# A second matmul operand that holds norm and shift in the second block of a two-block transformer, on one core

## The chip, the cores and the metric

The kernel runs on one core of a Trainium2 chip. The metric is the device time of one execution in microseconds (us), the median of several runs. TensorE (PE in the rows) multiplies, VectorE (DVE), ScalarE (ACT) and GpSimd (POOL) work on vectors, and SyncE (SP) issues most DMA transfers.

## What is computed

Two transformer blocks run one after the other on 256 tokens of width 1024, with all numbers in float32. The change touches the second block alone. Cut to what matters, that block is:

```python
def rms_norm(x, w):
    y = xf * lax.rsqrt(jnp.mean(xf * xf, axis=-1, keepdims=True) + EPS)
    return y * w
def modulate(h, shift, scale):
    return h * (1.0 + scale[:, None, :]) + shift[:, None, :]

for layer in range(2):
    mod = silu_c @ ada_w[layer] + ada_b[layer]
    shift_m, scale_m, gate_m, shift_f, scale_f, gate_f = jnp.split(mod, 6, axis=-1)
    h = modulate(rms_norm(x, norm_mix_w[layer]), shift_m, scale_m)
    # layer 0: neighbourhood attention and a gated recurrence (HGRN2) of h @ ev_w_in
    # layer 1: (gate_b * dwconv3(gate_c * u)) of h @ od_w_in
    y = even_mixer(h, ...) if layer == 0 else short_conv_mixer(h, ...)
    x = x + gate_m[:, None, :] * y
    h = modulate(rms_norm(x, norm_ffn_w[layer]), shift_f, scale_f)
    a, val = jnp.split(h @ ffn_w_up[layer], 2, axis=-1)      # 2 x 2816 columns
    x = x + gate_f[:, None, :] * ((gelu(dwconv3(a)) * val) @ ffn_w_down[layer])
```

So four stages begin with a normed, scaled and shifted activation h that is multiplied by a wide weight matrix.

## The kernel before

Activations lie with the model width on the partitions: x is eight blocks (kt) of 128 rows by 256 tokens. A float32 product is made of three fast ones: both operands are split into a high half and a low remainder, and `mm3` (L117) multiplies high by high (L122), high by low (L123) and low by high (L124). `proj_fm` (L135) makes one output tile of 128 features: 8 kt by 3 are 24 matmuls into one PSUM bank. `load_w` (L105) brings the tile's weights, 128 x 1024, by a DMA of SP into one of four buffers; ACT casts the high half (L114) and DVE subtracts for the low half (L115), into one of three buffers named w.

The operand of the tiles (x2, from `hl_tiles`, two buffers) is not h. It holds x times the gain, without the norm, so that PE can start while the sum of squares is still under way; two further columns, 256 and 257, hold the shift and half of it (`put_shift`). A tile therefore has 258 columns. The norm comes behind the product: DVE multiplies the 258 columns by rstd (1 / root mean square, the same in all 128 rows; 1 in the last two columns), and a later instruction adds column 256 as a bias. rstd is copied from PSUM by ACT (L233).

The four stages and their tiles in program order are: mix2 (32 tiles; the first eight are the forget gates of four heads and two directions, L928 and L979, whose logarithms, scans and exponentials, L476, L1018 to L1058, are made together after the last of them), ffn2(0) (22 steps ft of two tiles, the gate g and the up-product u, L378 to L401), mix3 (8 steps of three tiles, L1270 to L1291) and ffn2(1) (as ffn2(0)). ada vectors (`ada_after`; 96 rows of w_ada, one DVE instruction each, L450) are made in between at a written pace. A scheduler with a timing model of its own sets each engine's order of instructions ahead of the run; each engine then works its row off in order. The PSUM banks that serve the tiles (three named acc, two named sc) and the three buffers of w decide how far tiles run ahead.

Of the kernel before, what the change touches and what calls it, by code (L numbers as in the profile page):

```python
# [16 lines left out]
P = 128  # L17
# [8 lines left out]
DOWN = ((0, 8), (8, 8), (16, 6))  # L26

# [23 lines left out]
def network(ctx: ExitStack, tc: tile.TileContext, a):  # L51
# [107 lines left out]
    def hl_tiles():  # L159
        return HL.of(hpool.tile([P, 2, KT, S + 2], F32R, tag="x2", name="x2"))  # L160
# [208 lines left out]
    def ffn(pool, w_up, w_dn, x2, rstd, conv, mod, down_evac, rates):  # L369


        n = S + 2 if mod else S
        a2 = HL.of(pool.tile([P, 2, FT, S], F32R, name="a2"))
        for ft in range(FT):
            pg = proj_fm(w_up[ft, 0], x2, n)
            pu = proj_fm(w_up[ft, 1], x2, n)
            g = pool.tile([P, S + 2], F32, tag="g", bufs=2, name="g")
            nc.vector.tensor_tensor(out=g[:, :n], in0=pg[:, :n], in1=rstd[:, :n], op=ALU.mult)  # L378
            cv = pool.tile([P, S], F32, tag="cv", bufs=2, name="cv")
            if mod:  # L380
# [22 lines left out]
            if rates[0] and ft % rates[0] == rates[0] - 1:  # L403
# [514 lines left out]
    for kt in range(KT):  # L918
        nc.vector.scalar_tensor_tensor(out=x[:, kt], in0=x[:, kt], scalar=col("final_g", kt),
                                       in1=rx[:, :S], op0=ALU.mult, op1=ALU.mult)  # L920

    NM = S + 2
    with tc.tile_pool(name="mix2", bufs=1, reuse_waits="tile") as pool:
# [24 lines left out]
        y2 = hl_tiles()  # L948
# [22 lines left out]
        class Head:  # L971
# [16 lines left out]
            def project(self):  # L988
# [4 lines left out]
                gated(raw(12 + h), self.hq)  # L993
                t = raw(24 + h)
                plus_shift(t, t[:, :S])
                to_tokens(t[:, :S], self.v)
                gated(raw(28 + h), self.gg)
# [212 lines left out]
    def ffn2(l, gain, rates):  # L1210
        nxt = hl_tiles() if gain is not None else None
        sq = SumSq()

# [26 lines left out]
        def down_evac(nt, ps):  # L1240
            if not nxt:
                return final_evac(nt, ps)
            if nt == 0:
                gain_of(col("norm_mix_w_2", 8, 8), m(1, 1), gain)
                put_shift(nxt, m(1, 0))
# [4 lines left out]
            split(nxt, nt, x[:, nt], gain[:, nt : nt + 1])  # L1250
# [13 lines left out]
    with tc.tile_pool(name="mix3", bufs=1, reuse_waits="tile") as pool:  # L1264
# [7 lines left out]

        for ft in range(KT):
            tc_ = raw3(8 + ft)
            tu = raw3(16 + ft)
            nc.scalar.activation(tu[:, :S], tu[:, :S], AF.Identity, bias=tu[:, S : S + 1])
            cu = pool.tile([P, S], F32, tag="cu", bufs=2, name="cu")
            nc.vector.scalar_tensor_tensor(out=cu, in0=tc_[:, :S], scalar=tc_[:, S : S + 1],
                                           in1=tu[:, :S], op0=ALU.add, op1=ALU.mult)
# [3 lines left out]
            for i, so, si in ((0, slice(1, S), slice(0, S - 1)), (2, slice(0, S - 1), slice(1, S))):  # L1283
# [118 lines left out]
```

## Time and profile before

| | |
|---|---|
| time, median of 3 runs (lowest, highest) | 1372.6 us (1370.77, 1374.56) |
| the profiled execution: own time, span | 1373.04 us, 1371.3 us |
| PE, DVE, ACT, POOL busy | 98%, 82%, 61%, 4% |
| chain that ended last | PE 93% |
| mean granted clock of TensorE | 0.997 |

The span is what the trace covers of the execution; the rest of its own time lies around it. A busy share is the time in which an instruction of the engine runs over the span. The chain is followed back from the last instruction to whatever released it. Start times in rows are microseconds from the span's start.

### The profile page before, as it was taken

The page shows a single profiled execution, that of the slowest core. Times are in us where ns is not written, and L with a number is a line of the kernel's source. Part 1 is how long each engine was busy: PE and PEld are TensorE (multiplying, and loading weights), DVE is VectorE, ACT ScalarE, POOL GpSimd, SP SyncE. Part 2 cuts the span into 40 slices and gives each one's busy share as a digit, 9 for nine tenths or more (in the row PEclk, how much of TensorE's full clock was granted, in tenths as well). Part 3 has the DMA queues.
Part 4 walks back from the last instruction along what each step waited for, and adds up shares of the span by engine and source line. Part 5 has one row for each costly group of instructions (what it writes and reads, how often), then busy time and mean ns, then how long its engine had stood idle before and what let it go on. Part 6 is the DMA issues. An engine that isn't in the chain of part 4 may idle for free.

```text
span 1371.3 us, 26850 instructions
## 1 busy us (share of the span) xinstructions
PE 1342.9 (98%) x10482; PEld 1283.1 (94%) x10482; DVE 1119.4 (82%) x2125; ACT 829.9 (61%) x1444; POOL 51.0 (4%) x72
## 2 busy tenths in 40 slices
PE   8999999999999999999998999999999999999997
PEld 7998999999999999999898987899998999999986
DVE  7887799997775968999888976789989898888854
ACT  7756665555566765555557766666654455666653
POOL 1000000000101000000030110000000000000000
PEclk9999999999999999999999999999999999999999
DMA  7753667766655557888875453367779875656563
GB/s 261 249 176 109 221 224 223 228 208 195 207 161 156 197 186 250 279 271 275 269 232 179 148 166 122 125 216 231 227 221 324 288 248 187 195 184 185 177 185 100
DMA packets 79696, 284.19 MB, mean 207 GB/s; under 512 B 8912, under 2 KB 9040, under 8 KB 79440
## 3 DMA queue, kind: packets, MB, share of 16 engines
q1 hardware_dynamic: 78480, 278.67, 62.8%
q0 software_dynamic: 800, 3.15, 0.7%
q8 instruction: 82, 1.34, 0.4%
q10 hardware_dynamic: 288, 0.66, 0.1%
q14 instruction: 46, 0.38, 0.1%
HBM read 281.39 MB, written 1.05 MB: 206 GB/s over the span
## 4 chain that ended last, share of the span: by engine, by line
PE 93%; DVE 2%; ACT 2%; DMA 1%; issue 1%; SPq 0%; POOLq 0%; POOL 0%; DVEq 0%; ACTq 0%
PE ps_acc L124 15%; PE ps_acc L122 15%; PE ps_acc L123 14%; PE ps_sc L124 7%; PE ps_sc L122 7%; PE ps_sc L123 7%; PE ps_acc L129 6%; PE ps_sc L129 4%; PE ps_acc L130 3%; PE ps_sc L130 2%; PE ps_sc L304 2%; PE ps_acc L156 1%; PE ps_acc L154 1%; PE ps_acc L155 1%; PE ps_att L343 1%
## 5 line engine op out<-in xcount | busy, mean ns | idle before, releaser
L114 ACT CAST w<-wraw 128x1024 fp32r<-128x1024 f32 (+2 forms) x438 | 445.7, 1023 | 400.1 <-PE ps_acc L124 152.9
L115 DVE TENSOR_TENSOR w<-wraw,w 128x1024 fp32r<-128x1024 f32 (+2 forms) x438 | 522.8, 1198 | 123.1 <-ACT w L114 119.1
L124 PE MATMUL ps_acc<-x,w 128*128 128x256 f32 (+1 forms) x1560 | 441.6, 284 | 3.2 <-DVE w L115 3.2
L122 PE MATMUL ps_acc<-x,w 128*128 128x256 f32 (+1 forms) x1560 | 442.1, 285 | 2.5 <-ACT w L114 1.7
L123 PE MATMUL ps_acc<-x,w 128*128 128x256 f32 (+1 forms) x1560 | 441.6, 283 | 0.0
L122 PEld LDWEIGHTS ps_acc<-x,w 128*128 128x128 f32 x1560 | 294.2, 189 | 6.8 <-ACT w L114 3.6
L124 PEld LDWEIGHTS ps_acc<-x,w 128*128 128x128 f32 x1560 | 294.3, 189 | 6.3 <-DVE w L115 4.2
L123 PEld LDWEIGHTS ps_acc<-x,w 128*128 128x128 f32 x1560 | 295.3, 189 | 2.3 <-issue 2.0
L122 PE MATMUL ps_sc<-x,w 128*128 128x256 f32 (+1 forms) x840 | 240.0, 286 | 8.9 <-ACT w L114 6.7
L124 PE MATMUL ps_sc<-x,w 128*128 128x256 f32 (+1 forms) x840 | 239.5, 285 | 0.0
L123 PE MATMUL ps_sc<-x,w 128*128 128x256 f32 (+1 forms) x840 | 239.0, 285 | 0.2 <-DVE x L170 0.2
L122 PEld LDWEIGHTS ps_sc<-x,w 128*128 128x128 f32 x840 | 160.3, 191 | 10.8 <-ACT w L114 7.3
L123 PEld LDWEIGHTS ps_sc<-x,w 128*128 128x128 f32 x840 | 160.7, 191 | 0.8 <-DVE x L166 0.4
L124 PEld LDWEIGHTS ps_sc<-x,w 128*128 128x128 f32 x840 | 160.3, 191 | 0.3 <-DVE w L115 0.2
L129 PE MATMUL ps_acc<-a,w 128*128 128x512 f32 x374 | 130.8, 390 | 0.0
L450 DVE CUSTOM_DVE_ANT_0 ada<-ada,cvec,vec 128x1024 f32<-128x1024 f32 x96 | 121.8, 1277 | 2.4 <-DMA ada<-w_ada 2.3
L130 PE MATMUL ps_acc<-a,w 128*128 128x256 f32 x374 | 105.7, 283 | 1.3 <-DVE w L115 1.3
L129 PE MATMUL ps_sc<-a,w 128*128 128x512 f32 x242 | 84.9, 390 | 0.0
L129 PEld LDWEIGHTS ps_acc<-a,w 128*128 128x128 f32 x374 | 70.2, 188 | 14.4
L389 DVE SCALAR_TENSOR_TENSOR cv<-g,vec,cv 128x255 f32<-128x255 f32 (+1 forms) x176 | 83.0, 476 | 0.4 <-ACT cv L387 0.3
L130 PEld LDWEIGHTS ps_acc<-a,w 128*128 128x128 f32 x374 | 70.6, 189 | 2.4 <-DVE w L115 2.0
L130 PE MATMUL ps_sc<-a,w 128*128 128x256 f32 x242 | 68.2, 282 | 0.0
(377 smaller groups left out, 1893.4 us busy)
## 6 DMA issues: line engine op xcount, KB each, us to landing
wraw<-w_up SPq DMA_DIRECT2D x176, 512.0 KB, 4.3
ada<-w_ada SPq DMA_DIRECT2D x96, 512.0 KB, 4.8
wraw<-w_dn SPq DMA_DIRECT2D x64, 512.0 KB, 4.2
wraw<-w_ev SPq DMA_DIRECT2D x44, 512.0 KB, 3.8
wraw<-w_dn SPq DMA_DIRECT2D x32, 384.0 KB, 4.1
wraw<-w_od SPq DMA_DIRECT2D x24, 512.0 KB, 4.4
wraw<-w_qk SPq DMA_DIRECT2D x12, 512.0 KB, 4.8
wraw<-w_aout SPq DMA_DIRECT2D x8, 512.0 KB, 3.6
```

The lines of the kernel that those rows point to most:

```text
L114: nc.scalar.copy(hi[:, c], raw[:, c])
L115: nc.vector.tensor_tensor(out=lo[:, c], in0=raw[:, c], in1=hi.bitcast(F32)[:, c], op=ALU.subtract)
L122: nc.tensor.matmul(ps, w.h[:, c], x.h[:, kt, :n], start=first, stop=False)
L123: nc.tensor.matmul(ps, w.h[:, c], x.l[:, kt, :n], start=False, stop=False)
L124: nc.tensor.matmul(ps, w.l[:, c], x.h[:, kt, :n], start=False, stop=last)
L129: nc.tensor.matmul(ps, w.h[:, c], x.both[:, :, kt, :n], start=first, stop=False)
L130: nc.tensor.matmul(ps[:, 0], w.l[:, c], x.h[:, kt, :n], start=False, stop=last)
L154: nc.tensor.matmul(ps, x.l[:, kt, t], v.h[:, c], start=kt == 0, stop=False)
L155: nc.tensor.matmul(ps, x.h[:, kt, t], v.h[:, c], start=False, stop=False)
L304: nc.tensor.matmul(sps[j][:, o : o + n], self.q[r, qt * P : (qt + 1) * P], kap[r], start=True, stop=True)
L389: nc.vector.scalar_tensor_tensor(out=cv[:, so], in0=g[:, si], scalar=conv(i, ft), in1=cv[:, so], op0=ALU.mult, op1=ALU.add)
L450: nc.vector.tensor_tensor_reduce(out=out, in0=wt, in1=cvec[j], scale=1.0, scalar=col("ada_b", 48 * l + n), op0=ALU.mult, op1=ALU.add, accu ...
```

## The change

Four stages get a second operand, xn, that holds norm, gain and shift already. `normed` makes it, one block kt per step: POOL multiplies x by rstd into a buffer nt (two of them), ACT applies gain and shift in place, ACT casts the high half and DVE subtracts for the low half. The first tiles of a stage still read x2 with 258 columns and are normed behind the product: eight in mix2, six in each of the others (RAW = 3). All later tiles read xn with 256 columns and are evacuated straight from PSUM: no multiplication by rstd, no bias. The steps of `normed` are written behind the first tiles: two after each head's forget gates, three after each of the first three ft, four after each of the first two steps of mix3. Operand rows stand 260 apart. In mix2 the eight instructions that turn x into x times final_g times its own norm move behind the steps of `normed`, since these read the x from before. In the up-projection of ffn2(0) one ada vector less is made.

The diff, cut to its core (line numbers of the kernel after are larger; L126 to L128 are the three matmuls, L118 and L119 cast and subtraction of the weights, L191, L192, L169 and L170 the four instructions of `normed`):

```diff
@@ -24,6 +24,10 @@
+
+SX = 260
+
+RAW = 3
...
@@ -157,7 +161,7 @@
     def hl_tiles():
-        return HL.of(hpool.tile([P, 2, KT, S + 2], F32R, tag="x2", name="x2"))
+        return HL.of(hpool.tile([P, 2, KT, SX], F32R, tag="x2", name="x2"))
...
@@ -179,6 +183,17 @@
+    def normed(x2, src, gain, shift, rstd):
+
+        def step(kt):
+            t = npool.tile([P, S], F32, tag="sst", name="nt")
+            nc.gpsimd.tensor_tensor(out=t, in0=src[:, kt], in1=rstd[:, :S], op=ALU.mult)
+            nc.scalar.activation(t, t, AF.Identity, scale=gain[:, kt : kt + 1],
+                                 bias=shift[:, kt : kt + 1])
+            split(x2, kt, t)
+
+        return Fill([lambda kt=kt: step(kt) for kt in range(KT)])
...
@@ -366,19 +381,24 @@
         for ft in range(FT):
-            pg = proj_fm(w_up[ft, 0], x2, n)
-            pu = proj_fm(w_up[ft, 1], x2, n)
-            g = pool.tile([P, S + 2], F32, tag="g", bufs=2, name="g")
-            nc.vector.tensor_tensor(out=g[:, :n], in0=pg[:, :n], in1=rstd[:, :n], op=ALU.mult)
+            after = mod and ft >= RAW
+            n = S + 2 if mod and not after else S
+            pg = proj_fm(w_up[ft, 0], xn if after else x2, n)
+            pu = proj_fm(w_up[ft, 1], xn if after else x2, n)
+            if after:
+                g = pg
+            else:
+                g = pool.tile([P, S + 2], F32, tag="g", bufs=2, name="g")
+                nc.vector.tensor_tensor(out=g[:, :n], in0=pg[:, :n], in1=rstd[:, :n], op=ALU.mult)
             cv = pool.tile([P, S], F32, tag="cv", bufs=2, name="cv")
             if mod:
-                nc.scalar.activation(g[:, :S], g[:, :S], AF.Identity, bias=g[:, S : S + 1])
+                if not after:
+                    nc.scalar.activation(g[:, :S], g[:, :S], AF.Identity, bias=g[:, S : S + 1])
...
@@ -390,7 +410,7 @@
-            if mod:
+            if mod and not after:
                 u = pool.tile([P, S + 2], F32, tag="u", bufs=2, name="u")
                 nc.vector.tensor_tensor(out=u, in0=pu[:, :n], in1=rstd, op=ALU.mult)
...
@@ -400,7 +420,9 @@
-            if rates[0] and ft % rates[0] == rates[0] - 1:
+            if fill and not after:
+                fill(-(-KT // RAW))
+            elif rates[0] and ft % rates[0] == rates[0] - 1:
                 ada_after(last)
...
@@ -915,9 +937,8 @@
     rstd = rstd_of(v2)
     rx = rstd_of(v1)
-    for kt in range(KT):
-        nc.vector.scalar_tensor_tensor(out=x[:, kt], in0=x[:, kt], scalar=col("final_g", kt),
-                                       in1=rx[:, :S], op0=ALU.mult, op1=ALU.mult)
+    xn = hl_tiles()
+    norm = normed(xn, x, gains[:, 0], m(0, 0), rstd)
...
@@ -928,15 +949,21 @@
-        def plus_shift(t, out):
-            nc.scalar.activation(out, t[:, :S], AF.Identity, bias=t[:, S : S + 1])
...
+        def product(nt):
+            return proj_fm(a["w_ev"][nt], xn)[:, :S]
...
@@ -1140,14 +1164,12 @@
-            na_steps += [lambda nt=nt: plus_shift(raw(nt), nq[:, nt]),
-                         lambda nt=nt: plus_shift(raw(4 + nt), nk_[:, nt]),
+            na_steps += [lambda nt=nt: nc.scalar.copy(nq[:, nt], product(nt)),
+                         lambda nt=nt: nc.scalar.copy(nk_[:, nt], product(4 + nt)),
                          lambda nt=nt: na_value(nt)]
...
@@ -1180,6 +1202,11 @@
         for head in heads:
             sigmoid = head.forget()
+            norm(2)
+        y2 = hl_tiles()
+        for kt in range(KT):
+            nc.vector.scalar_tensor_tensor(out=x[:, kt], in0=x[:, kt], scalar=col("final_g", kt),
+                                           in1=rx[:, :S], op0=ALU.mult, op1=ALU.mult)
         with tc.issue_after(sigmoid.ins):
             for head in heads:
                 head.logs()
...
@@ -1208,8 +1235,10 @@
-        nxt = hl_tiles() if gain is not None else None
+        nxt = []
         sq = SumSq()
+        xn = hl_tiles()
+        norm = normed(xn, x, gains[:, 1 + 2 * l], m(l, 3), rstd)
...
@@ -1270,13 +1301,26 @@
+        xn = HL.of(pool.tile([P, 2, KT, S], F32R, name="xn"))
+        norm = normed(xn, x, gains[:, 2], m(1, 0), rstd)
+
+        def product(nt):
+            return proj_fm(a["w_od"][nt], xn)[:, :S]
+
         for ft in range(KT):
...
+            if ft < RAW - 1:
+                tc_ = raw3(8 + ft)
+                tu = raw3(16 + ft)
...
+                norm(4)
+            else:
+                pc = product(8 + ft)
+                tu = pool.tile([P, NM], F32, tag="od", bufs=4, name="od")
+                nc.scalar.copy(tu[:, :S], product(16 + ft))
+                nc.vector.tensor_tensor(out=cu, in0=pc, in1=tu[:, :S], op=ALU.mult)
```

The order of instructions moves with it. PE, the ninth tile of mix2 and what follows: before, each tile's 24 matmuls stand in one piece, here the end of tile 9110 and the start of 9143.

```order
L122 MATMUL ps_acc_9110<-x2_6482,w_9107 128x258
L123 MATMUL ps_acc_9110<-x2_6482,w_9107 128x258
L124 MATMUL ps_acc_9110<-x2_6482,w_9107 128x258
L122 MATMUL ps_acc_9143<-x2_6482,w_9140 128x258
L123 MATMUL ps_acc_9143<-x2_6482,w_9140 128x258
L124 MATMUL ps_acc_9143<-x2_6482,w_9140 128x258
```

After, the three tiles that follow the first eight (9151, 9182, 9213) are worked off together, one block of xn after the other; these nine rows are one of the last blocks:

```order
L126 MATMUL ps_acc_9151<-x2_8775,w_9148 128x256
L126 MATMUL ps_acc_9182<-x2_8775,w_9179 128x256
L126 MATMUL ps_acc_9213<-x2_8775,w_9210 128x256
L127 MATMUL ps_acc_9151<-x2_8775,w_9148 128x256
L128 MATMUL ps_acc_9151<-x2_8775,w_9148 128x256
L127 MATMUL ps_acc_9182<-x2_8775,w_9179 128x256
L128 MATMUL ps_acc_9182<-x2_8775,w_9179 128x256
L127 MATMUL ps_acc_9213<-x2_8775,w_9210 128x256
L128 MATMUL ps_acc_9213<-x2_8775,w_9210 128x256
```

What moved: no tile ends before the last block of xn is there, and all three buffers of w come free together. The same holds at the start of the other three stages, with other tile numbers.

ACT in mix2 behind the last forget gate: before, the logarithms, a cast of weights, then exponentials between evacuations of tiles (nq, nk).

```order
L979 ACTIVATE ke<-ev 128x256
L476 ACT_TABLE_LOAD
L476 ACTIVATE lf<-ke,lb 128x256 x8
L114 CAST w<-wraw 128x1024
L1024 ACT_TABLE_LOAD
L1024 ACTIVATE lf<-qd 128x256 x2
L932 ACTIVATE nq<-ev 128x256
L1024 ACTIVATE lf<-qd 128x256
```

After, the last three blocks of xn (8775) stand among logarithms and exponentials:

```order
L498 ACT_TABLE_LOAD
L498 ACTIVATE lf<-ke,lb 128x256 x8
L192 ACTIVATE nt<-nt,mod,gains 128x256
L169 CAST x_8775<-nt 128x256
L1048 ACT_TABLE_LOAD
L1048 ACTIVATE lf<-qd 128x256 x4
L169 CAST x_8775<-nt 128x256
L1049 ACTIVATE qd<-qd 128x256 x4
L192 ACTIVATE nt<-nt,mod,gains 128x256
L169 CAST x_8775<-nt 128x256
L1171 COPY nq<-ps_acc 128x256
L118 CAST w<-wraw 128x1024
```

What moved: the last cast of xn stands behind both tables, eight logarithms and eight exponentials. The next cast of weights follows behind the evacuation of the first of the three tiles (nq).

ACT in ffn2(0) behind the copy of rstd: before,

```order
L233 COPY rstd<-ps_att 128x256
L381 ACTIVATE g<-g 128x256
L114 CAST w<-wraw 128x1024
L387 ACTIVATE cv<-g,vec 128x256
L381 ACTIVATE g<-g 128x256
L387 ACTIVATE cv<-g,vec 128x256
L114 CAST w<-wraw 128x1024
L391 ACT_TABLE_LOAD
```

and after, with the blocks of xn (11021) threaded through:

```order
L248 COPY rstd<-ps_att 128x256
L192 ACTIVATE nt<-nt,mod,gains 128x256
L401 ACTIVATE g<-g 128x256
L169 CAST x_11021<-nt 128x256
L192 ACTIVATE nt<-nt,mod,gains 128x256
L118 CAST w<-wraw 128x1024
L407 ACTIVATE cv<-g,vec 128x256
L401 ACTIVATE g<-g 128x256
L169 CAST x_11021<-nt 128x256
```

What moved: the eight blocks of xn spread over the work on the first three ft; the last cast of xn stands 33 rows behind the copy of rstd, with three casts of weights, three g, three cv, three gelu with one table load and three casts of a among them.

## Rows read from the trace of the kernel before

**Rows 1.** The page, part 1: busy time, share and instructions of each engine.

```profile
PE 1342.9 (98%) x10482; PEld 1283.1 (94%) x10482; DVE 1119.4 (82%) x2125; ACT 829.9 (61%) x1444; POOL 51.0 (4%) x72
```

**Rows 2.** Windows: mix2 up to its output product, and ffn2(0)'s up-projection; columns named.

```profile
core 0: us, PE busy (x) PEld busy (x) DVE busy (x) ACT busy (x) POOL busy (x), PEclk, DMA share, GB/s
705.00:866.00 161.00, 154.86 (x1252) 140.60 (x1251) 125.14 (x313) 111.21 (x222) 27.11 (x32) 0.99 0.47 152
888.00:1016.00 128.00, 128.00 (x1067) 127.96 (x1066) 114.10 (x201) 84.23 (x136) 0.69 (x1) 1.00 0.71 224
```

**Rows 3.** Timeline of PE: starts of tiles, 256 columns, 258 columns, then down-projection.

```profile
169.53 0.28 PE L122 MATMUL ps_sc<-x,w 128*128 128x256 f32 x1
226.97 0.28 PE L122 MATMUL ps_sc<-x,w 128*128 128x256 f32 x1
...
903.21 0.28 PE L122 MATMUL ps_sc<-x,w 128*128 128x258 f32 x1
1009.88 0.28 PE L122 MATMUL ps_sc<-x,w 128*128 128x258 f32 x1
...
335.29 0.28 PE L122 MATMUL ps_acc<-a,w 128*128 128x256 f32 x1
342.99 0.28 PE L122 MATMUL ps_acc<-x,w 128*128 128x256 f32 x1
```

**Rows 4.** The page, part 5: matmuls of tiles, one of three lines, by kind of bank.

```profile
L124 PE MATMUL ps_acc<-x,w 128*128 128x256 f32 (+1 forms) x1560 | 441.6, 284 | 3.2 <-DVE w L115 3.2
...
L122 PE MATMUL ps_sc<-x,w 128*128 128x256 f32 (+1 forms) x840 | 240.0, 286 | 8.9 <-ACT w L114 6.7
```

**Rows 5.** Timeline of PE: where the first tile on xn would start, stage by stage.

```profile
733.90 0.28 PE L122 MATMUL ps_acc<-x,w 128*128 128x258 f32 x1
...
906.08 0.28 PE L122 MATMUL ps_acc<-x,w 128*128 128x258 f32 x1
...
1098.40 0.28 PE L122 MATMUL ps_acc<-x,w 128*128 128x258 f32 x1
...
1190.93 0.28 PE L122 MATMUL ps_sc<-x,w 128*128 128x258 f32 x1
```

**Rows 6.** Timeline of ACT in mix2 behind the last forget gate.

```profile
735.62 1.28 ACT L476 ACT_TABLE_LOAD   x1
736.92 4.05 ACT L476 ACTIVATE lf<-ke,lb 128x256 f32<-128x256 f32 x8
```

**Rows 7.** Timeline of ACT at the start of ffn2(0).

```profile
889.39 0.51 ACT L169 ACTIVATE x<-x,gains 128x256 fp32r<-128x256 f32 x1
...
894.70 2.00 ACT L114 CAST w<-wraw 128x1024 fp32r<-128x1024 f32 x2 [4.49 <-PE ps_sc L124]
...
898.40 0.37 ACT L233 COPY rstd<-ps_att 128x256 f32<-128x256 f32 x1
...
907.76 0.70 ACT L400 CAST a<-act 128x256 fp32r<-128x256 f32 x2
```

**Rows 8.** Timeline of DVE in mix3.

```profile
1092.62 0.75 DVE L1270 TENSOR_TENSOR od<-ps_acc,rstd 128x258 f32<-128x258 f32 x2
...
1101.27 1.28 DVE L450 CUSTOM_DVE_ANT_0 ada<-ada,cvec,vec 128x1024 f32<-128x1024 f32 x1
```

**Rows 9.** Windows around the first forget gates and around mix2's exponentials (columns as rows 2).

```profile
721.00:724.00 3.00, 0.92 (x7) 0.57 (x6) 2.05 (x6) 2.97 (x5) 0.60 (x1) 1.00 0.82 240
724.00:733.00 9.00, 9.00 (x65) 9.00 (x64) 6.83 (x16) 4.86 (x9) 0.00 (x0) 0.81 0.38 128
...
742.00:747.50 5.50, 4.04 (x34) 3.69 (x33) 5.50 (x15) 5.49 (x12) 0.00 (x0) 1.00 0.29 91
```

**Rows 10.** Timeline of POOL in mix2.

```profile
712.37 1.83 POOL L1160 TENSOR_TENSOR rpbt<-rpbt,win 128x768 f32<-128x768 f32 x1
```

**Rows 11.** Timeline of DVE over the same stretch.

```profile
712.97 2.31 DVE L115 TENSOR_TENSOR w<-wraw,w 128x1024 fp32r<-128x1024 f32 x1
...
715.91 1.22 DVE L115 TENSOR_TENSOR w<-wraw,w 128x1024 fp32r<-128x1024 f32 x1
```

More of the change, by code (lines that the diff above doesn't have):

```diff
@@ L929, in raw, with gated, to_sbuf @@
             return t
-        def plus_shift(t, out):
-            nc.scalar.activation(out, t[:, :S], AF.Identity, bias=t[:, S : S + 1])
-        def gated(t, out):
-            nc.scalar.activation(out, t[:, :S], AF.Tanh, scale=0.5, bias=t[:, S + 1 : S + 2])
-            nc.scalar.activation(t[:, :S], t[:, :S], AF.Identity, scale=0.5, bias=t[:, S + 1 : S + 2])
+        def product(nt):
+            return proj_fm(a["w_ev"][nt], xn)[:, :S]
+        def gated(ps, out):
+            t = pool.tile([P, NM], F32, tag="ev", bufs=3, name="ev")
+            nc.scalar.activation(out, ps, AF.Tanh, scale=0.5)
+            nc.scalar.mul(t[:, :S], ps, 0.5)
             nc.vector.scalar_tensor_tensor(out=out, in0=out, scalar=1.0, in1=t[:, :S],
                                            op0=ALU.add, op1=ALU.mult)
+        def to_sbuf(ps):
+            t = pool.tile([P, NM], F32, tag="ev", bufs=3, name="ev")
+            nc.scalar.copy(t[:, :S], ps)
+            return t[:, :S]
         def to_tokens(src, dst):
@@ L992, in project @@
                 self.v = pool.tile([P, 2, P], F32, tag="hgv", bufs=2, name="hgv")
[L993 to L997, printed above, removed]
+                gated(product(12 + h), self.hq)
+                to_tokens(to_sbuf(product(24 + h)), self.v)
+                gated(product(28 + h), self.gg)
             def gates(self):
@@ L1240, in down_evac @@
         def down_evac(nt, ps):
-            if not nxt:
+            if gain is None:
                 return final_evac(nt, ps)
             if nt == 0:
+                nxt.append(hl_tiles())
                 gain_of(col("norm_mix_w_2", 8, 8), m(1, 1), gain)
-                put_shift(nxt, m(1, 0))
+                put_shift(nxt[0], m(1, 0))
             for half in ps:
@@ L1249, in down_evac @@
                     op0=ALU.mult, op1=ALU.add)
-            split(nxt, nt, x[:, nt], gain[:, nt : nt + 1])
+            split(nxt[0], nt, x[:, nt], gain[:, nt : nt + 1])
             sq.add(x[:, nt])
@@ L1271, in raw3 @@
             return t
+        xn = HL.of(pool.tile([P, 2, KT, S], F32R, name="xn"))
+        norm = normed(xn, x, gains[:, 2], m(1, 0), rstd)
+        def product(nt):
+            return proj_fm(a["w_od"][nt], xn)[:, :S]
         for ft in range(KT):
[L1274 to L1276 removed]
             cu = pool.tile([P, S], F32, tag="cu", bufs=2, name="cu")
[L1278 to L1279 removed]
+            if ft < RAW - 1:
+                tc_ = raw3(8 + ft)
+                tu = raw3(16 + ft)
+                nc.scalar.activation(tu[:, :S], tu[:, :S], AF.Identity, bias=tu[:, S : S + 1])
+                nc.vector.scalar_tensor_tensor(out=cu, in0=tc_[:, :S], scalar=tc_[:, S : S + 1],
+                                               in1=tu[:, :S], op0=ALU.add, op1=ALU.mult)
+                norm(4)
[4 more added lines that the diff above has]
+                nc.vector.tensor_tensor(out=cu, in0=pc, in1=tu[:, :S], op=ALU.mult)
             cv = pool.tile([P, S], F32, tag="cv3", bufs=2, name="cv3")
@@ L1286, in network @@
                                                in1=cv[:, so], op0=ALU.mult, op1=ALU.add)
-            tb_ = raw3(ft)
-            last = nc.vector.scalar_tensor_tensor(out=cv, in0=tb_[:, :S], scalar=tb_[:, S : S + 1],
-                                                  in1=cv, op0=ALU.add, op1=ALU.mult)
+            if ft < RAW - 1:
+                tb_ = raw3(ft)
+                last = nc.vector.scalar_tensor_tensor(out=cv, in0=tb_[:, :S],
+                                                      scalar=tb_[:, S : S + 1],
+                                                      in1=cv, op0=ALU.add, op1=ALU.mult)
+            else:
+                last = nc.vector.tensor_tensor(out=cv, in0=product(ft), in1=cv, op=ALU.mult)
             split(y2, ft, cv)
```

13 lines of the change are left out of this document (5 added, 8 removed).

## The prediction, made before the changed kernel ran

> **What bounds the kernel now.** I read the page's busy shares first: PE runs 1342.9 us of the span [rows 1], so 1371.3 - 1342.9 = 28.4 us is all the idle time that PE has. Then the windows of the stages that change: the up-projection of ffn2(0) has PE busy 128.00 of 128.00 us, while mix2 leaves 161.00 - 154.86 = 6.1 us idle [rows 2]. So in the ffn stages only fewer or faster matmuls make time, and every wait of PE that is new is added whole; in mix2 a little could also come from shorter waits. Last I read the timeline of PE around the four places where the change swaps operands [rows 5], and what ACT and DVE do there [rows 6 to 8].
>
> **What the matmuls give.** Before, 32 + 44 + 24 + 44 = 144 tiles of 24 matmuls have 258 columns. After, 24 + 38 + 18 + 38 = 118 of them have 256: 118 x 24 = 2832 matmuls. The pace is read between two starts of tiles with no idle time between. With 256 columns: 226.97 - 169.53 = 57.44 us over 20 tiles, 480 matmuls, 119.7 ns each. With 258: 1009.88 - 903.21 = 106.67 us over 37 tiles, 888 matmuls, 120.1 ns [rows 3]. The difference, 0.45 ns, gives 2832 x 0.45 = 1.3 us. By columns alone, two of 258 of 120.1 ns would be 0.93 ns and 2.6 us. The far bound is the last tile's part of a down-projection, whose operand rows stand 256 apart: 342.99 - 335.29 = 7.70 us over 66 matmuls, 116.7 ns, which would make 2832 x 3.4 = 9.6 us [rows 3]. I take -2 us: the row of 256 columns is the same kind of tile with the same operand layout, and its rows were 258 apart, as before the change. The Trainium skill, "TensorE: Matmul & The Clock Gate", section "Back-to-back issue gap", gives for an isolated matmul N / 2.4 + 2.5 ns, 109.2 and 110.0 ns for 256 and 258 columns; the trace's 119.7 and 120.1 do not agree in level, and by the page's difference of 0.83 ns the term would be an estimated -2.4 us.
>
> **What is taken from DVE and ACT.** Per ft of an ffn that reads xn, DVE loses the products of g and u with rstd (0.42 us each, as in [rows 8], where two in a row take 0.75): 0.84 us, 32 us over 38 ft. Mix2 and mix3 lose 24 + 18 of them, 42 x 0.42 = 18 us. That is worth nothing where PE was never idle [rows 2]; in mix2 it could shorten what is left of the 6.1 us after the two idle stretches that I name below, 721 to 724 with 2.08 and 742 to 747.5 with 1.46 [rows 9]: 6.1 - 2.1 - 1.5 = 2.6 us at most. I take 0. The ada vector left out (1.28 us on DVE [rows 8]) is made later; DVE has room. The eight products with final_g keep their size; what they make is read again only behind mix2's output product, some 100 us later. The buffers also cost nothing: xn takes the one that y2 or the next x2 held before, and these are now allocated once the first tiles have freed theirs (733.9 in mix2 [rows 5]), ahead of their first writers. On SP no transfer is added, and the four raw weights buffers are full whenever PE waits for xn; were that cover gone, a transfer of weights would be late by its own few us at each swap.
>
> **What is added.** Four times eight blocks of: a product on POOL, an activation and a cast on ACT, a subtraction on DVE. No such POOL product is in the trace; the nearest has 768 columns and took 1.83 us [rows 10]. A third of it, 0.61, bounds a product of 256 columns from below and the whole from above; I take 0.7, near the third, since the work per column is the same kind. On ACT the activation takes 0.51 alone and some 0.41 in a row, since neighbours overlap by 0.1 (two casts of weights of 1.05 take 2.00, two casts of 256 columns of 0.40 take 0.70, so 0.31 for a further one) [rows 7]. On DVE the subtraction takes 0.33 in a row [rows 8]. Per block that is 0.7 on POOL, 0.72 on ACT and 0.33 on DVE, and per stage 5.8 us of ACT. None of it is a bound by its sum. What decides is when the last block is ready, since by the order the first three tiles on xn end only with it. Without a wait they would end 3 x 2.88 = 8.64 us behind their start: at 742.5, 914.7, 1107.0 and 1199.6 [rows 5].
>
> **Mix2.** The last cast of xn stands on ACT behind both tables and all logarithms and exponentials. The table load at 735.62 comes some 0.4 later, behind one more activation of xn; the logarithms then end at 740.97 + 0.4 = 741.4 [rows 6]. Behind them by the order: one activation and three casts (0.41 + 3 x 0.31), the second table (1.28, as the first [rows 6]), eight exponentials of 0.35 (as the casts of 256 columns), one more activation (0.41): 5.8 us, so 747.2. Hand-overs between POOL, ACT and DVE, and DVE's own row (four products, scans and decays ahead of the last subtraction), add 0.3 to 0.5 at each of three steps: I put the last low half at 748.5, the tiles' end 0.7 later, with six matmuls: 749.2, 6.7 late. Then all three buffers of w come free together: the next tile needs a cast of 1.05 [rows 7] and a subtraction of 1.22 [rows 11], less what PE can do between, so some 2 us more. Of this 1.46 us is a wait that before had at 742 to 747.5 [rows 9] and that falls away. 6.7 + 2 - 1.5 = 7.2. The clock comes on top: PE would be idle for most of 740 to 752, and in before, behind a stretch with PE busy 0.92 of 3.00 us, the granted clock was 0.81 over 9.00 us [rows 9], which is 1.7 us lost to the lower level. +9 in all, between 5 and 13.
>
> **ffn2(0).** rstd is there at 898.40 + 0.37. Up to the last cast of xn, by the order, ACT has 3 casts of weights (2.9), 8 activations and 8 casts (5.8), 3 g, 3 cv and 3 gelu (0.41, 0.5 and 0.35: 3.8), a table load (1.28) and 3 casts of a (0.9): 14.7 us, 913.4 if it never waits. With some 1.5 of waits (g and u need their tiles) and the subtraction of 0.42 it is 915.4, tiles end at 916.1, 1.4 late; with the restart of 1.8, +3.2 (1.5 to 6).
>
> **Mix3.** Here DVE's row is the later one. From 1092.62 [rows 8] up to the last subtraction of xn it holds 15 products and subtractions of 0.34, 8 of 0.40 with three operands, 3 subtractions of weights of 1.14 and 2 ada vectors of 1.28: 14.3 us, 1106.9, and with 0.9 of waits 1107.8. Tiles end at 1108.5, 1.5 late; with the restart +3.4 (1.5 to 6).
>
> **ffn2(1)** is ffn2(0) without the table load: 1.4 - 1.28 leaves 0.1 of the delay, which I set to 0; the restart stays, +1.7 (0.5 to 4). Sum: 9 + 3.2 + 3.4 + 1.7 - 2 = +15.3. The profiled execution took 1373.04 us, 0.4 over the median of 1372.6; 1373.0 + 15.3 = 1388.3, so **1388 us**. With all bounds but the far pace it lies between 1378 and 1398.
>
> **The rivals.**
> *Hidden:* the blocks of xn are ready early enough that three tiles in turn cover them, and the next weights are cast in time. For it: ACT is busy for only 84.23 of 128.00 us in the up-projection [rows 2]. Against it: the order puts the three tiles' ends behind the last block, and before mix2's last block ACT has work without a gap up to 747. Then only the columns count: 1373 - 2 = 1371 us.
> *Faster matmuls, the other sign:* operand rows 260 apart bring the down-projection's pace of 116.7 ns, and not to the 2832 matmuls alone: every operand of the kernel gets the new spacing, so 3 x (1560 + 840) = 7200 matmuls [rows 4] gain 119.7 - 116.7 = 3.0 ns, 21.6 us, beside the 1.3 us for columns. With the waits as summed that is 1373 + 17.3 - 22.9 = 1367 us. It decides from 17.3 us on, 2.2 ns per matmul of the 7200. For it: two paces for 256 columns stand in the trace, and the operands differ in spacing. Against it: with rows 258 apart every second row starts at another multiple than its neighbour, and over the 888 matmuls between the two starts I see no step in the pace from row to row.
> *POOL holds DVE:* in before a subtraction of weights took 2.31 us while POOL ran a product of 1.83, and 1.22 with POOL on an instruction that has no second tensor [rows 10, 11]: 1.09 us lost to 1.83. Eight products of 0.7 that each cost DVE 0.6 of their time are 3.4 us a stage; in the three stages where a late block decides, +10 to 11: 1399 us. Against it: POOL works one product per 1.4 us at most here and DVE has gaps. The Trainium skill, "SBUF — State Buffer", section "Who interferes with whom", calls the port pair that DVE and GpSimd share an exclusive lock; the trace's 2.31 against 1.22 agrees.
>
> **How the numbers follow.** Waits as summed 0.65, POOL's hold on top 0.08, hidden 0.14, faster matmuls 0.13. About 4 us (0.3%) is what a measurement can tell from no change here. Of the waits 0.01 to 0.02 falls below 1377, so that faster is 0.13 + 0.01, same 0.14 + 0.01 and slower the rest: faster 0.14, same 0.15, slower 0.71. The range 1370 to 1400 takes in the hidden case and POOL's; it leaves out the faster matmuls (0.13) and a tail above of 0.05.
>
> **What would show it.** In the trace after: three tiles at each swap whose matmuls come in groups of nine, with gaps in front that name the cast or the subtraction of xn (L169, L170); a gap behind them that names the weights (L118, L119); a granted clock below 1 in mix2 between 740 and 755; a pace near 119.5 ns for tiles on xn; POOL's L191 near 0.7 us. No gaps at the swaps would refute the waits; a pace under 118 ns would refute the -2; subtractions of weights of 2 us beside L191 would speak for POOL's hold. Wrong outright I would be if the chip ran the blocks of xn much earlier than the sums of ACT and DVE allow, or if a wait that I read as unchanged (the four attention pairs of mix2) moved with the new order.

## The result, and the profile after

The changed kernel takes 1383.1 us (median of 4 runs, 1381.7 to 1385.5), beside 1371.8 us of the kernel before in the same runs: a ratio of 1.008, interval 1.0066 to 1.0094. It is slower by 11.3 us; the forecast was slower by 15.3, 1388 us in 1370 to 1400.

Page of the kernel after, its head and part 1, which answer to [rows 1]: PE has lost a share of the span, though its instructions are as many.

```profile
span 1383.8 us, 26776 instructions
...
PE 1341.3 (97%) x10482; PEld 1277.6 (92%) x10482; DVE 1099.0 (79%) x2039; ACT 830.7 (60%) x1470; POOL 80.0 (6%) x104
```

Windows of three stretches, each from one copy of rstd to the next (mix2, ffn2(0), mix3), in the kernel before; columns as in [rows 2]:

```profile
721.88:898.40 176.52, 170.18 (x1376) 154.84 (x1375) 131.79 (x328) 120.78 (x243) 13.17 (x13) 0.99 0.45 145
898.40:1090.64 192.24, 189.80 (x1438) 182.66 (x1437) 172.33 (x292) 113.06 (x175) 0.69 (x1) 1.00 0.79 257
1090.64:1183.24 92.60, 92.60 (x777) 92.60 (x776) 79.72 (x136) 49.90 (x75) 0.69 (x1) 1.00 0.66 211
```

and in the kernel after:

```profile
715.74:896.91 181.17, 170.88 (x1376) 154.78 (x1375) 127.04 (x311) 122.43 (x257) 19.64 (x21) 0.96 0.44 138
896.91:1091.88 194.97, 191.58 (x1438) 183.67 (x1437) 164.02 (x261) 109.58 (x174) 7.99 (x9) 0.98 0.75 254
1091.88:1190.17 98.29, 93.08 (x777) 91.89 (x776) 80.52 (x128) 55.38 (x91) 8.21 (x9) 1.00 0.64 206
```

The stretches carry more than the whole difference. The part ahead of mix2's rstd, in which the diff alters only the spacing of rows, ends at 715.74 in place of 721.88: 6.1 us are gained there. Mix2 loses 4.7, ffn2(0) 2.7, mix3 5.7, and the rest from 1183.24 and 1190.17 to the end of the spans 188.1 against 193.6, 5.6. Sum: +12.5, the difference of the spans. So two large terms of opposite sign stand behind a moderate sum.

Timeline of PE after the change, the rows at the four swaps in which PE had been idle (in brackets the idle time and what ended it):

```profile
736.15 0.62 PE L126 MATMUL ps_acc<-x,w 128*128 128x256 f32 x3 [2.76 <-ACT x L169]
...
737.29 0.39 PE L127 MATMUL ps_acc<-x,w 128*128 128x256 f32 x1 [0.52 <-DVE x L170]
...
739.09 1.01 PE L126 MATMUL ps_acc<-x,w 128*128 128x256 f32 x3 [0.83 <-ACT x L169]
...
742.70 0.58 PE L127 MATMUL ps_acc<-x,w 128*128 128x256 f32 x1 [0.27 <-DVE x L170]
...
744.90 0.58 PE L126 MATMUL ps_acc<-x,w 128*128 128x256 f32 x1 [0.55 <-ACT w L118]
...
908.70 0.39 PE L126 MATMUL ps_acc<-x,w 128*128 128x256 f32 x1 [1.46 <-ACT w L118]
...
918.55 0.38 PE L126 MATMUL ps_acc<-x,w 128*128 128x256 f32 x1 [1.12 <-ACT w L118]
...
919.50 0.58 PE L126 MATMUL ps_sc<-x,w 128*128 128x256 f32 x1 [0.45 <-ACT w L118]
...
1107.03 0.39 PE L127 MATMUL ps_acc<-xn,w 128*128 128x256 f32 x1 [0.90 <-DVE xn L170]
...
1111.15 0.39 PE L127 MATMUL ps_acc<-xn,w 128*128 128x256 f32 x1 [1.50 <-DVE xn L170]
...
1113.85 0.38 PE L126 MATMUL ps_acc<-xn,w 128*128 128x256 f32 x1 [0.67 <-ACT w L118]
...
1115.06 0.38 PE L126 MATMUL ps_sc<-xn,w 128*128 128x256 f32 x1 [0.72 <-ACT w L118]
...
1207.52 0.39 PE L126 MATMUL ps_sc<-x,w 128*128 128x256 f32 x1 [0.70 <-ACT x L169]
...
1211.32 0.38 PE L126 MATMUL ps_acc<-x,w 128*128 128x256 f32 x1 [1.12 <-ACT w L118]
...
1212.27 0.39 PE L126 MATMUL ps_acc<-x,w 128*128 128x256 f32 x1 [0.45 <-ACT w L118]
```

Every swap waits for a block of xn or, behind the three tiles that end together, for weights. In ffn2(0) all three waits are for weights: the cast for the first, at 908.70, stands on ACT behind casts of xn, a table load and other work on the first ft.

Windows of the kernel after around the swaps (ffn2(0), mix3, ffn2(1), mix2), of 20 us each:

```profile
906.00:926.00 20.00, 16.84 (x107) 15.69 (x107) 17.23 (x32) 15.54 (x31) 3.42 (x4) 0.83 0.49 159
...
1098.00:1118.00 20.00, 14.79 (x115) 13.60 (x114) 17.91 (x31) 12.26 (x24) 4.35 (x5) 1.00 0.51 158
1200.00:1220.00 20.00, 16.54 (x112) 15.17 (x112) 15.78 (x28) 13.23 (x27) 4.01 (x4) 0.91 0.41 131
735.00:755.00 20.00, 16.64 (x95) 14.30 (x96) 15.40 (x49) 14.35 (x34) 0.74 (x1) 0.74 0.37 130
```

In 906 to 926 PE is idle for 3.16 us only, yet issues 107 matmuls, where the undisturbed 20 us that follow hold 173: 66 matmuls fewer at 117 ns are 7.7 us. The granted clock of 0.83 takes 0.17 x 20 = 3.4 us of that; the 1.1 us that are left stand in longer steps from matmul to matmul around the waits. The clock is below 1 in three of the four windows.

Timeline of PE after, starts of tiles 19 apart (456 matmuls, first block) and 27 apart (648, ffn2(0) on xn), which answer to [rows 3]:

```profile
170.76 0.28 PE L126 MATMUL ps_acc<-x,w 128*128 128x256 f32 x1
...
224.31 0.28 PE L126 MATMUL ps_sc<-x,w 128*128 128x256 f32 x1
...
932.20 0.28 PE L126 MATMUL ps_acc<-x,w 128*128 128x256 f32 x1
...
1008.34 0.28 PE L126 MATMUL ps_sc<-x,w 128*128 128x256 f32 x1
```

53.55 / 456 = 117.4 ns and 76.14 / 648 = 117.5 ns: 2.3 and 2.6 ns under the 119.7 and 120.1 of before.

### The profile page after: what moved, and what is told of

It is laid out like the page before. It is cut to its first block, busy times and chain, and to the rows that moved or that the text cites. A ratio compares the mean times of both kernels' runs of the same rounds, so it can differ in the third digit from the quotient of the medians.

```text
span 1383.8 us, 26776 instructions
## 1 busy us (share of the span) xinstructions
PE 1341.3 (97%) x10482; PEld 1277.6 (92%) x10482; DVE 1099.0 (79%) x2039; ACT 830.7 (60%) x1470; POOL 80.0 (6%) x104
## 5 line engine op out<-in xcount | busy, mean ns | idle before, releaser
L118 ACT CAST w<-wraw 128x1024 fp32r<-128x1024 f32 (+2 forms) x438 | 445.0, 1022 | 324.4 <-PE ps_acc L128 112.0
L119 DVE TENSOR_TENSOR w<-wraw,w 128x1024 fp32r<-128x1024 f32 (+2 forms) x438 | 523.7, 1200 | 134.1 <-ACT w L118 130.8
L126 PE MATMUL ps_acc<-x,w 128*128 128x256 f32 (+1 forms) x1472 | 417.0, 286 | 11.3 <-ACT w L118 6.7
L127 PE MATMUL ps_acc<-x,w 128*128 128x256 f32 (+1 forms) x1472 | 417.2, 284 | 0.8 <-DVE x L170 0.8
L128 PE MATMUL ps_acc<-x,w 128*128 128x256 f32 (+1 forms) x1472 | 415.8, 284 | 1.4 <-DVE w L119 1.2
L126 PEld LDWEIGHTS ps_acc<-x,w 128*128 128x128 f32 x1472 | 278.9, 190 | 18.9 <-ACT w L118 9.8
L128 PEld LDWEIGHTS ps_acc<-x,w 128*128 128x128 f32 x1472 | 280.1, 191 | 3.8 <-DVE w L119 2.3
L127 PEld LDWEIGHTS ps_acc<-x,w 128*128 128x128 f32 x1472 | 280.4, 191 | 2.9 <-DVE x L170 1.6
L126 PE MATMUL ps_sc<-x,w 128*128 128x256 f32 (+1 forms) x784 | 223.1, 285 | 10.1 <-ACT w L118 7.0
L127 PE MATMUL ps_sc<-x,w 128*128 128x256 f32 (+1 forms) x784 | 223.2, 285 | 0.2 <-DVE x L174 0.2
L128 PE MATMUL ps_sc<-x,w 128*128 128x256 f32 (+1 forms) x784 | 222.3, 284 | 1.1 <-DVE w L119 1.1
L126 PEld LDWEIGHTS ps_sc<-x,w 128*128 128x128 f32 x784 | 149.4, 191 | 12.4 <-ACT w L118 8.1
L128 PEld LDWEIGHTS ps_sc<-x,w 128*128 128x128 f32 x784 | 149.9, 191 | 1.7 <-DVE w L119 1.6
L127 PEld LDWEIGHTS ps_sc<-x,w 128*128 128x128 f32 x784 | 149.8, 191 | 1.1 <-DVE x L170 0.6
L239 POOL TENSOR_TENSOR rt<-v,neghalf 128x2 f32<-128x2 f32 x11 | 10.0, 907 | 770.1 <-DVE v L226 724.0
```

The lines of the kernel that those rows point to most:

```text
L118: nc.scalar.copy(hi[:, c], raw[:, c])
L119: nc.vector.tensor_tensor(out=lo[:, c], in0=raw[:, c], in1=hi.bitcast(F32)[:, c], op=ALU.subtract)
L126: nc.tensor.matmul(ps, w.h[:, c], x.h[:, kt, :n], start=first, stop=False)
L127: nc.tensor.matmul(ps, w.h[:, c], x.l[:, kt, :n], start=False, stop=False)
L128: nc.tensor.matmul(ps, w.l[:, c], x.h[:, kt, :n], start=False, stop=last)
L239: nc.gpsimd.tensor_tensor(out=rt, in0=v, in1=neghalf[:, :2], op=ALU.pow)
```

## The experiments

Theory 1 after the result: the spacing of rows speeds up all 7200 matmuls. Theory 2: late blocks of xn at the swaps cost what was lost. Paces below are read as above, between starts of undisturbed tiles.

**Rows 260 apart and nothing else**, in the kernel before:

```diff
-        return HL.of(hpool.tile([P, 2, KT, S + 2], F32R, tag="x2", name="x2"))
+        return HL.of(hpool.tile([P, 2, KT, 260], F32R, tag="x2", name="x2"))
```

> The kernel before with operand rows 260 apart and nothing else. Theory 1 (spacing): the pace of the tiles goes from 119.7 to 117.4 ns in the whole kernel, 7200 matmuls of it, so about 1372 - 16 = 1356 us. Rival (the first block's 6.1 us came from another order or from what the second operand moved): 1370 to 1372 us, pace still 119.7 ns.

1368.4 us, ratio 0.9965 (0.9952 to 0.9978): a gain, but a quarter of what theory 1 gave. The starts of two tiles of ffn2(0), 23 tiles and 552 matmuls apart, say why:

```profile
931.47 0.28 PE L122 MATMUL ps_sc<-x,w 128*128 128x258 f32 x1
...
998.47 0.28 PE L122 MATMUL ps_sc<-x,w 128*128 128x258 f32 x1
```

67.00 / 552 = 121.4 ns. With 256 columns the pace is 117.4 as in the change; with 258 the same spacing makes it slower, 121.4 against 120.1. Theory 3 takes the place of theory 1: spacing and columns count together. 3744 matmuls gain 2.25 ns and 3456 lose 1.3, -8.4 + 4.5 = -3.9 us; -3.8 was measured. The parts agree less well than the sum. Ahead of mix2's rstd (715.82 in this run) 6.1 us are gained, where 3408 of the matmuls would give 7.7; behind it 1.8 are lost, where 3.6 are summed. And undisturbed tiles with 258 columns in mix2 take 119.8 ns here, not 121.4, which theory 3 does not explain.

**The change with rows 258 apart** (SX = S + 2):

> The change with operand rows 258 apart. Theory 1 (spacing): the 16 us are gone, 1383 + 16 = 1399 us, and the copy of rstd that begins mix2 comes at about 722 in place of 715.7. Rival (the pace comes from the 256 columns or from the order): 1383 us.

1391.4 us, 1.0135 (1.012 to 1.015); rstd of mix2 at 721.39. 8.3 us above the change, not 16: xn's tiles, now 256 columns in rows 258 apart, run at 118.9 ns in the ffn stages, 1.4 more than with 260. In mix3 xn is allocated apart, with rows 256 apart in both runs, so that 2832 - 432 = 2400 matmuls lose 1.4 ns, 3.4 us, beside some 6 of the first block and less 624 x 1.3 = 0.8 us for the tiles with 258 columns: 8.6 us.

**Rows 262 apart** in the kernel before:

> The kernel before with rows 262 apart: 1048 bytes, as 1032 no multiple of 16, while 1040 is one. If the pace hangs on rows that begin at a multiple of 16 bytes: no change, 1372 us, 119.7 ns. Rival (any spacing but 258 helps, say by where the two halves come to lie): about 1356 us.

1371.4 us, 0.9997 (0.9986 to 1.0009), no change; 119.2 ns with 256 columns, 120.0 with 258.

**Six ft in place of three on the operand without norm** (five steps in mix3):

```diff
-RAW = 3
+RAW = 6
```

> The change with the first six ft (five steps in mix3) on the operand without norm, in place of three (two). Theory 2 (the blocks of xn are late, 19 to 20 us behind rstd): in both ffn and in mix3 the 6.5 to 7.3 us that each loses around the swap go, mix2 keeps its loss; 1383 - 20 = 1363 us. Rival (the cost is the added work itself, POOL holding DVE, and falls wherever the blocks are made): 1378 to 1383 us.

1367.2 us, 0.9956 (0.9939 to 0.9972): 16 us under the change and 5 under before. ffn2(0) takes 188.3 us from rstd to rstd, mix3 94.8 (92.6 before), and mix2 keeps its 180.7. The window of ffn2(0) in which the change had 107 matmuls:

```profile
906.00:926.00 20.00, 20.00 (x168) 20.00 (x168) 19.20 (x35) 17.68 (x36) 3.99 (x4) 1.00 0.63 194
```

No idle time and full clock, though blocks of xn are made there, with four of POOL's eight products in the window. The last low half even comes later, 27.6 us behind rstd where the change has 19.5, and PE does not wait for it. So the added work costs next to nothing in ffn2(0) where the tiles on xn come late enough. The run changes two things at once, though: PE now also works off each tile in one piece, and what the order block by block costs by itself is not separated.

**Four ft, and six tiles of mix2** (in this run and the others with six tiles of mix2, y2's buffer is also allocated later, since x2 is read longer):

```diff
-RAW = 3
+RAW = 4
...
+        left = [6]
         def product(nt):
+            if left[0]:
+                left[0] -= 1
+                t = raw(nt)[:, :S + 1]
+                nc.scalar.activation(t[:, :S], t[:, :S], AF.Identity, bias=t[:, S : S + 1])
+                return t[:, :S]
```

> As the run before it with four ft in place of six (three steps in place of five in mix3). Theory 2: the blocks of xn come 19 to 20 us behind rstd and the third late tile would end some 16 us behind it with three ft, 22 with four: the wait is gone but for 1 us a stage, two and a half fewer tiles per stage pay 121.4 ns; 1361 to 1364 us. Rival (added work, not lateness): the same time as with six, within 1 us, or with three, 1380.

1379.7 us, 1.0053 (1.0036 to 1.0071): a miss. The three tiles still end together by the scheduler's order, and PE waits 1.11 and 0.44 us for the next weights behind them, with 0.94 and 0.57 ahead: ffn2(0) takes 192.3 us. One ft more removes only a part of the wait. That the order block by block is what has to go is likely, since with six ft it is gone and so is the wait, but no run changes it alone.

**Six ft, and six tiles of mix2:**

> As the run with six ft on the operand without norm (1367.2 us), and in mix2 six further tiles read it too. Theory 2 (late blocks): mix2, 180.65 us from copy of rstd to copy of rstd there, falls to 174 to 176; 1361 to 1362 us. Rival (mix2's loss is the additional work of ACT ahead of the exponentials, on the path of the recurrence, not the tiles' wait): mix2 stays at 179 or more, 1366 us.

1370.3 us, 0.9977 (0.9967 to 0.9987): a miss as well. The swap's waits in mix2 are gone; 0.41 and 1.43 us for weights are left, on tiles of the operand without norm, where before had 1.46. Yet the stretch takes 181.3 us. New waits stand later; PE's timeline there:

```profile
797.99 0.43 PE L233 MATMUL ps_att<-ident,ov 128*128 128x128 f32 x2 [1.37 <-POOL ov L1153]
...
801.21 0.58 PE L126 MATMUL ps_acc<-x,w 128*128 128x256 f32 x1 [2.56 <-ACT ev L966]
```

The second one is new in kind: PE waits for a bank that ACT evacuates (L966 halves a gate's product out of PSUM). Before the change DVE emptied the bank with the product by rstd. Around the two waits the granted clock is 0.66, over 797 to 807.

**The same, and in mix2 DVE copies each tile on xn out of PSUM** ahead of ACT (the diff at the gates; the other tiles of mix2 likewise):

```diff
-            nc.scalar.activation(out, ps, AF.Tanh, scale=0.5)
-            nc.scalar.mul(t[:, :S], ps, 0.5)
+            nc.vector.tensor_copy(out=t[:, :S], in_=ps)
+            nc.scalar.activation(out, t[:, :S], AF.Tanh, scale=0.5)
+            nc.scalar.mul(t[:, :S], t[:, :S], 0.5)
```

> As the run with six ft and six tiles of mix2 on the operand without norm (1370.3 us), and in mix2 a tile on xn leaves PSUM by one copy of DVE; ACT then works from SBUF, as before the change. Theory 4 (mix2 still loses 5 us there since the banks wait for ACT, which evacuates them behind its other work: 2.6 and 1.4 us of waits near 800 us): mix2 falls from 181.3 to 177 us or less, 1366 us. Rival (the new order of the scheduler, whichever engine evacuates): mix2 stays above 180, 1370 us.

1363.4 us, 0.993 (0.9916 to 0.9945), the lowest median of all: mix2 falls from 181.3 to 177.2 us, both waits near 800 are gone, and the granted clock over 793 to 803 is 1.00. In turn the waits for weights near 737 grow from 1.84 to 3.55 us. So the work that was taken from DVE in mix2 was what emptied that bank in time. Since the scheduler also ordered anew, the one wait is shown, not each of the 4.1 us.

**The product with rstd on DVE in place of POOL:**

> The change with the product of x and rstd on DVE in place of POOL (0.34 us in a row there, 32 of them). Theory 2: what makes the blocks late is the ring of two buffers through four steps and the other work ahead of each, so a POOL step less gains little: 1380 to 1383 us. Rival (POOL holds DVE while it reads, or is slow itself): the blocks are ready 3 us or more earlier in each stage and the time falls by 8 us or more, to 1375 or less.

1384.8 us, 1.0085 (1.0067 to 1.0103): as the change. This does not tell how much POOL's hold on DVE costs, since DVE takes on 8 x 0.34 = 2.7 us of products a stage in its place. The last low halves come 26.8, 19.3, 20.1 and 18.2 us behind rstd, in the change 26.9, 19.5, 19.9 and 19.0. That there is a hold shows in the change where a subtraction of weights and a product of POOL overlap (first DVE, then POOL):

```profile
729.78 1.75 DVE L119 TENSOR_TENSOR w<-wraw,w 128x1024 fp32r<-128x1024 f32 x1
```
```profile
729.54 0.91 POOL L191 TENSOR_TENSOR nt<-x,rstd 128x256 f32<-128x256 f32 x1 [0.36 <-DVE x L170]
```

1.75 against 1.22 us [rows 11]: DVE lost 0.53 of the 0.67 us for which the two overlap. The Trainium skill, "SBUF — State Buffer", section "Who interferes with whom", calls the port pair that the two engines share an exclusive lock; the trace agrees but for 0.14 us. In mix3 the hold lies on the way to the last block (DVE beside a product of POOL, and the same instruction without one):

```profile
1097.63 0.47 DVE L1316 SCALAR_TENSOR_TENSOR cu<-od 128x256 f32<-128x256 f32 x1
...
1101.00 0.96 DVE L1316 SCALAR_TENSOR_TENSOR cu<-od 128x256 f32<-128x256 f32 x1
```
```profile
1100.76 0.92 POOL L191 TENSOR_TENSOR nt<-x,rstd 128x256 f32<-128x256 f32 x1 [1.50 <-DVE xn L170]
```

Summed over DVE's rows beside L191, each against the same instruction elsewhere, the loss is 1.5 us in mix2, 1.6 in ffn2(0), 2.9 in mix3 and 1.5 in ffn2(1).

**Six and six, rows 264 apart:**

> As the first of these four with rows 264 apart, 1056 bytes, a multiple of 16 and of 32. Theory 3 (256 columns are read faster where a row begins at a multiple of 16 bytes): the pace is as with 260, 117.4 ns or less for 256 columns, and the time the same within 2 us. Rival (something about 260 alone): pace of 119 to 120 ns and some 10 us more.

1373.3 us, 1.001 (0.9999 to 1.002), 2.9 above the same with 260; 118.3 ns with 256 columns. The pace is better than with 258 (119.7), but 260 gives 117.4. The tiles with 258 columns take 119.8 ns here, though a row begins at a multiple of 16 bytes as with 260 (121.4). So a start at such a multiple explains neither pace by itself.

**260 for operands of 256 columns, 258 for the four that hold the shift**, in the kernel before:

> The kernel before with rows 260 apart for operands read with 256 columns, and 258 apart, as before, for the four that hold the shift and are read with 258. Theory 3 (256 columns gain from a start at a multiple of 16 bytes, 258 columns lose by it): 7200 - 3456 = 3744 matmuls gain 2.25 ns and the 3456 lose nothing, 1372 - 8.4 = 1363.7 us, 4.6 us under the run with 260 throughout. Rival (the second block lost in that run by something else than the spacing): 1368 us.

1368.7 us, 0.9967 (0.9954 to 0.9979): a miss, no better than 260 throughout. The paces are as expected, 117.4 and 120.1 ns, and the three stretches behind mix2 are together 3.3 us shorter (191.2, 92.5 and 181.9 us against 192.4, 93.1 and 183.4 up to PE's last instruction). They were lost at the start of mix2: there some 90 matmuls that stood ahead of its rstd now stand behind it. PE's first tile of mix2 shows what it waits for:

```profile
703.65 0.39 PE L122 MATMUL ps_sc<-x,w 128*128 128x258 f32 x1 [4.21 <-ACT x L181]
```

L181 is ACT's cast of the columns that hold the shift. With 260 throughout the first such cast ran at 511.40, here at 703.39, and the granted clock over 700 to 715 is 0.77 in place of 1.00. Why the scheduler moved that cast stays open.

**xn in the two ffn alone, from the seventh ft on**, and the same **with 258 for the operands that hold the shift**:

> The second operand in the two ffn alone, from the seventh ft on; mix2 and mix3 as before; rows 260 apart. By the stretches of other runs: 1368.4 us (rows 260 alone) less 192.4 - 188.3 and 183.4 - 180.3 us: 1361.2 us. Rival (the time that mix2 lost with xn was moved there from elsewhere and comes back): 1366 us or more.

> As the run before it, with the operands that hold the shift 258 apart: their 32 + 24 + 24 tiles, 1920 matmuls, go from 121.4 back to 120.1 ns, 2.5 us: 1358.7 us. Rival as there: 1361 us or more.

1364.4 us, 0.9939 (0.9925 to 0.9954), and 1367.6 us, 0.9956 (0.9942 to 0.9971): both above what was expected, 3.2 and 8.9 us. The ffn stretches are as expected (187.9 and 180.4 us in the first), but mix3, whose code is that of before, takes 97.2 us against 93.1 with rows 260 alone. DVE's timeline at its output product in the first of the two, and the window around it:

```profile
1147.99 1.27 DVE L472 CUSTOM_DVE_ANT_0 ada<-ada,cvec,vec 128x1024 f32<-128x1024 f32 x1
...
1149.59 1.27 DVE L472 CUSTOM_DVE_ANT_0 ada<-ada,cvec,vec 128x1024 f32<-128x1024 f32 x1
```
```profile
1150.00:1160.00 10.00, 8.24 (x56) 7.84 (x55) 10.00 (x19) 6.11 (x13) 0.00 (x0) 0.83 0.48 158
```

With six ft the steps of normed displace three ada vectors in place of one; two of the late ones are made here, where DVE has no room (10.00 of 10.00 us), PE waits 2.0 us for weights, and the clock falls to 0.83. The second run starts mix2 as the run with 260 and 258 did, with PE waiting 4.21 us for the cast of the shift columns.

## Why the prediction came out as it did

**Right in sum: the waits.** The last low half of xn in mix2 was put 748.5 - 721.88 = 26.6 us behind the copy of rstd. It came at 742.22 + 0.42, 26.9 us behind 715.74. PE's idle time at the swaps was forecast as 7.2, 3.2, 3.4 and 1.7 us over before, 15.5 in all. Measured: 4.93 - 1.46 = 3.47 in mix2, 3.16 in ffn2(0), 5.21 in mix3 and 3.46 in ffn2(1), 15.3. That the sum fits is in part luck, since the parts do not: in mix2 part of the wait shows as slow clock, and in the other stages the last low half came 19.5, 19.9 and 19.0 us behind rstd, 2.5 to 3.3 later than I added up. In mix3 it ended at 1111.36 + 0.41, 19.9 us behind rstd where 17.2 were summed. DVE's row held what I counted and it idled for 0.58 us only, less than the 0.9 that I gave it. What was mis-sized are its instructions: five of them beside POOL's products took some 2.3 us longer than the same elsewhere.

**Mis-sized: the clock.** I charged 1.7 us, in mix2 alone. By the windows of 20 us above, the granted clock takes 0.26 x 20 = 5.2 us in mix2, part of it while PE was idle, 3.4 in ffn2(0), nothing in mix3 and 1.8 in ffn2(1): 10.4 in all, where before had 1.7 [rows 9], so up to 8.7 us more. It fell in the ffn stages where PE had idled for 0.45 to 1.46 us at a time; at the lower level (1.2 in place of 2.4 GHz) matmuls with 256 columns stand 213 ns apart. In mix3, idle gaps of 0.90, 1.50, 0.67 and 0.72 us left it at 1.00. Some 3 us more, an estimate from what the stretches lose beside idle time, clock and pace, were lost at full clock: behind a wait the first matmul is 0.22 us ahead of the next, not 0.12.

**Mis-sized: the matmuls.** "I take -2 us" failed by more than 10 us: the -2 was read from rows 258 apart, which the change does not keep. The gain is 6.1 us ahead of mix2, 2832 x 2.6 = 7.4 for xn's tiles, less 624 x 1.3 = 0.8 for the tiles with 258 columns: 12.7 us. What failed is the argument against the rival of faster matmuls. I looked for a step from row to row in the stream of 258 columns, where there is none. In the stream of 256 columns of the same trace it stands: over undisturbed tiles between 170 and 280 us, the three matmuls on a block take 116.7 to 118.9 ns each on even blocks and 121.7 to 122.8 on the first three odd ones, whose rows begin at an odd multiple of 8 bytes from the operand's start; the last block, which ends with the change of tile, takes 117.4. After the change the first seven blocks lie between 116.4 and 118.9, and the last takes 115.0. That the start of a row makes the step is not shown: xn with rows 258 apart, in the change, has no such order in ffn2(0), 118.0 to 120.6 on its first seven blocks. The rival's gain was there, rather more than half its size.

**Missed, small: DVE's relief.** I took 0. In before PE waited 1.30 us for weights in ffn2(0)'s down-projection and 0.78 at 1084.80; after the change neither wait is there. The second is gone with rows 260 alone as well, so at most the first speaks for the relief. The two terms that were too small, clock and matmuls, nearly cancelled: 1383 came out under 1388 by luck as much as by the sum.

**POOL's hold: real, smaller than the rival had it.** DVE lost 1.5 to 2.9 us a stage to it, where the rival had 3.4, and in mix3 it is most of what I missed. POOL's product took 0.73 to 0.93 us where it ran singly, 0.94 in the mean of all 32, with 0.7 in the forecast. One reading behind the rival was wrong. The subtraction of 1.22 us at 715.91 did not run beside an instruction without a second tensor; from 716.07 on POOL had a product with one:

```profile
716.07 2.76 POOL L1160 TENSOR_TENSOR rpbt<-rpbt,win 128x768 f32<-128x768 f32 x1
```

DVE had begun first and lost nothing; POOL took 2.76 us, where the same product took 1.83 at 712.37. In the cases shown in which DVE lost time, POOL had begun first.

**A sum that was off.** The bounds of the five terms, 5 to 13, 1.5 to 6, 1.5 to 6, 0.5 to 4 and -2.6 to -1.3, give 1379 to 1401 us, not 1378 to 1398. The result lies within either.

**What stays open:** why 260 is faster than 264, and why 258 columns are slower with 260 than with 258 in three stages but not in mix2; what POOL's hold costs in the kernel's time; what the order block by block costs without the lateness; and what of mix2's remaining 1 to 2 us is the scheduler's order.

## What to carry to other kernels

Take the pace of a matmul stream from the trace for each pair of columns and row spacing, and look for a step between rows in each stream by itself: here two numbers of a tile's shape moved the pace of 7200 matmuls by 1 to 2%, up or down. When an operand is made later, count the tiles that can run until it is there by the chip's own chain (19 to 27 us here), and see that the tiles behind are not worked off together, or the weights' buffers come free at one time. Before work is taken off an engine with time to spare, ask what it released: DVE's product emptied the PSUM banks.

## What the runs showed of the hardware that was not expected

Pace of a float32-replacement matmul with a moving operand of 128 rows, by spacing of operand rows: 256 columns take 119.7 ns at 258 (118.9 for xn in the ffn stages of the change with rows 258 apart), 117.4 at 260, 119.2 at 262, 118.3 at 264, and 116.7 at 256 [rows 3] (117.7 for xn in mix3); 258 columns take 120.1 at 258, 121.4 at 260 (119.8 in mix2 of the kernel before with rows 260 apart), 120.0 at 262 and 119.8 at 264. So spacing and columns move the pace, and something else beside them that no run here isolates. Around idle gaps of only 1.46, 1.12 and 0.45 us the granted clock was 0.83 over the 20 us from 906; around gaps of 0.90, 1.50, 0.67 and 0.72 us it was 1.00 over the 20 us from 1098. And where a POOL product that had begun first overlapped a DVE instruction on two tensors by 0.67 us, DVE took 0.53 us longer.
